# Gates' running sums as rows of the logits' second product; the gated products dealt over six heads

## The chip, the cores and the metric

The kernel runs on one core of a Trainium2 chip. The time is device time in microseconds (us) for one execution; the number compared is the median of several runs. The core has a matrix engine (TensorE, PE in the profile, with PEld for its weight loads), VectorE (DVE), ScalarE (ACT), GpSimd (POOL), and queues that issue DMA transfers (SP's is the one used most). Each engine takes its instructions in the order in which the built kernel has them.

## The reference

One decoder block over a sequence of 1024 tokens and width 1024: forgetting attention with 8 heads of 64, beside a spatial gating branch in chunks of 128 tokens, then a gated feed-forward with a causal convolution. What the change touches is the attention's logits and the branch's output product:

```python
c = jnp.cumsum(log_f, axis=1)                      # running sums of the forget gates, per head
logits = jnp.einsum('bqhd,bkhd->bhqk', qi, k).astype(jnp.float32) * scale
logits = logits + ci[..., None] - c_k
causal = pi[:, None] >= key_pos[None, :]
logits = jnp.where(causal, logits, -jnp.inf)
p = jax.nn.softmax(logits, axis=-1)
...
mix = jnp.concatenate([att, sg], axis=-1)          # sg: the gated branch
h = h + mix @ w_out[layer]
```

The term of the query's own position falls out of the softmax, so the kernel adds only the key's.

## The kernel before

Matrix products are made in a 32-bit format of reduced precision from operands that are split into a high and a low half (`hi`, `lo`); a product is then the sum of three. ScalarE usually makes the high half (`act.copy`, L154 in `split_w`) and VectorE or GpSimd the low half (L160: source minus high half). A product of 512 columns with four blocks of weights is 12 matmuls.

The program runs in this order:

- Input products for the gated branch and the values.
- Four steps of query and key products (`qk_step`, i = 0 to 3; TensorE's line is L402 in `product`), each with weights (`Weights`) whose sums S1 to S4 GpSimd makes (L424 to L426, L432). Queries and keys are stored to DRAM (`qd`, `kd`, L534). Beside the steps run the norm of the gate (`gate_part`: square on ScalarE, reduce, root, reciprocal, and two products with `gms` on VectorE) and the forget gates: `forget`, `forget_sums` and `turn`. These share two small tiles of the tag `gg` (`c` and `r`; two buffers), a tag from which the weights' sum S2 also takes its buffer. `turn`, called at the end of step 0, transposes the running sums on TensorE (L518), copies them negated into `rows`, a part of `c`, and stores them to `ncd` (L520).
- Values and spatial gating; `turn_sg` (L705 to L708) turns the gated branch with TensorE transposes, copies on ScalarE (L707) and subtractions on VectorE (L708).
- The attention, heads 0 to 7. `head_loads` brings the operands of a head two heads ahead. `logits(h, j)` makes a block of 128 queries: two matmuls for up to 512 keys each (L796, L797), then one VectorE reduction (L798) that adds the row `ck`, limits, and finds the minimum `mn`, and an exponential on ScalarE (L800). `ck` is the running sum of the head, broadcast by DMA to 128 partitions; before each block GpSimd sets the keys after the query to a large number in it (affine select, L790). `turn_p` transposes the weights (L813) and splits them (ScalarE L814, VectorE L815), and `values` multiplies them with V (L832, L840, L841). `row_tail` inverts the row sums (L738, L739, L741), and `pair_half` normalizes a pair of heads on GpSimd (L752 to L754; on VectorE for the last pair).
- The gated branch's output product, `sg_out`, is a generator of 16 products (two halves of the weights `wos` by 8 token tiles; TensorE L874 to L876, VectorE L877). The table `FILLS` says after which step (head, step) one product is taken; key (-1, j) is after the logits' block j of head 0, which is made before any step. They lie between the attention's matmuls as filling. The second half's weights are split when the eighth product is done.
- Output product of the attention, for which GpSimd splits weights during the last heads (`wo_load`), and the feed-forward, which is most of the time and not touched.

The scheduler that orders each engine's instructions works from its own estimates; an `after` call fixes one instruction behind another. Before, GpSimd's normalizations and weight splits are fixed behind chosen selects (`sels`).

## Time and profile before

| | |
|---|---|
| median of 3 runs | 1076.82 us (1076.59 to 1077.02) |
| profiled execution | 1076.44 us |
| its span in the trace | 1074.7 us |
| mean granted TensorE clock | 0.998 of full |
| TensorE busy | 1054.8 us, 5013 instructions |
| VectorE busy | 892.9 us, 1303 instructions |
| ScalarE busy | 571.0 us, 985 instructions |
| GpSimd busy | 237.2 us, 219 instructions |

The profile lists the busy time of each engine, the busy shares in slices, the chain of work that ended last, and the costliest groups of instructions with the idle time before them and who ended it. In a timeline row stand the start in us from the span's start, the length (of the whole run of x instructions), engine, line, operation, output tile and input tile with shapes, how many, and in brackets the engine's idle time just before and what ended it. A wait row has engine and line, what was waited for, the total in us, how often, and the longest. PE's matmuls are pipelined: one of 512 columns takes 0.39 us from end to end, but the next starts after 0.23 us.

### The profile page before, as it was taken

The page shows a single profiled execution, that of the slowest core. Times are in us where ns is not written, and L with a number is a line of the kernel's source. Part 1 is how long each engine was busy: PE and PEld are TensorE (multiplying, and loading weights), DVE is VectorE, ACT ScalarE, POOL GpSimd, SP SyncE. Part 2 cuts the span into 40 slices and gives each one's busy share as a digit, 9 for nine tenths or more (in the row PEclk, how much of TensorE's full clock was granted, in tenths as well). Part 3 has the DMA queues.
Part 4 walks back from the last instruction along what each step waited for, and adds up shares of the span by engine and source line. Part 5 has one row for each costly group of instructions (what it writes and reads, how often), then busy time and mean ns, then how long its engine had stood idle before and what let it go on. Part 6 is the DMA issues. An engine that isn't in the chain of part 4 may idle for free.

```text
span 1074.7 us, 14461 instructions
## 1 busy us (share of the span) xinstructions
PE 1054.8 (98%) x5013; PEld 875.8 (81%) x5013; DVE 892.9 (83%) x1303; ACT 571.0 (53%) x985; POOL 237.2 (22%) x219
## 2 busy tenths in 40 slices
PE   9999999989999899999999999999999999999997
PEld 6888788778888788878888888888888888888886
DVE  5985798777777869999899999989988776898774
ACT  6666644456666845764444444444444444454653
POOL 0002134020223651054333333333322000000000
PEclk9999999999999999999999999999999999999999
DMA  9242257957556335132244523223331899433442
GB/s 338 97 140 97 68 159 213 265 165 215 162 177 225 120 128 185 72 118 97 98 137 161 172 69 127 99 98 99 107 118 46 289 327 319 123 95 97 140 125 96
DMA packets 66297, 160.80 MB, mean 150 GB/s; under 512 B 7976, under 2 KB 8240, under 8 KB 66224
## 3 DMA queue, kind: packets, MB, share of 16 engines
q1 hardware_dynamic: 65792, 159.32, 45.5%
q8 instruction: 39, 0.64, 0.2%
q10 hardware_dynamic: 432, 0.57, 0.1%
q14 instruction: 34, 0.28, 0.1%
HBM read 117.06 MB, written 42.80 MB: 149 GB/s over the span
## 4 chain that ended last, share of the span: by engine, by line
PE 74%; DVE 2%; issue 2%; DMA 2%; ACT 2%; POOL 0%; DVEq 0%; ACTq 0%; POOLq 0%; SPq 0%
PE k L1369 19%; PE qa L1117 11%; PE qc L1117 11%; PE qd L1117 11%; PE qb L1117 5%; PE pb L832 2%; PE pb L813 2%; PE pf L874 1%; PE pf L876 1%; PE pf L875 1%; PE pl L796 1%; PE pl L797 1%; DMA raw<-wos 1%; PE pb L1026 1%; PE pb L1028 1%
## 5 line engine op out<-in xcount | busy, mean ns | idle before, releaser
L1369 PE MATMUL k<-whb,wha 128*128 128x512 f32 x924 | 209.7, 389 | 0.0
L1369 PEld LDWEIGHTS k<-whb,wha 128*128 128x128 f32 x924 | 173.3, 188 | 36.2 <-DVE wha L160 0.2
L1117 PE MATMUL qc<-xT,whb 128*128 128x512 f32 x540 | 129.8, 389 | 0.0
L1117 PE MATMUL qa<-xB,wha 128*128 128x512 f32 x528 | 127.2, 390 | 0.0
L1117 PEld LDWEIGHTS qc<-xT,whb 128*128 128x128 f32 x540 | 101.3, 188 | 21.2 <-ACT whb L154 0.2
L1117 PEld LDWEIGHTS qa<-xB,wha 128*128 128x128 f32 x528 | 98.8, 188 | 20.8 <-DVE wha L160 0.4
L154 ACT CAST wha<-sg 128x512 fp32r<-128x512 f32 x77 | 47.7, 622 | 96.9 <-PE k L1369 86.6
L154 ACT CAST whb<-sg 128x512 fp32r<-128x512 f32 x82 | 50.6, 618 | 85.8 <-PE qc L1117 68.5
L160 DVE TENSOR_TENSOR wha<-sg,wha 128x512 fp32r<-128x512 f32 x77 | 52.8, 688 | 41.0 <-ACT wha L154 40.9
L1117 PE MATMUL qd<-xB,whb 128*128 128x512 f32 x264 | 63.8, 389 | 0.5 <-DVE h L1236 0.5
L1117 PE MATMUL qd<-xT,whb 128*128 128x512 f32 x264 | 63.6, 389 | 0.0
L815 DVE TENSOR_TENSOR pt<-pb,pt 128x512 fp32r<-128x512 f32 (+1 forms) x80 | 50.0, 635 | 14.5 <-ACT pt L814 13.4
L160 DVE TENSOR_TENSOR whb<-sg,whb 128x512 fp32r<-128x512 f32 x82 | 58.3, 711 | 4.4 <-ACT whb L154 4.3
L1117 PE MATMUL qb<-xT,whb 128*128 128x512 f32 x252 | 60.8, 389 | 0.0
L1004 POOL TENSOR_TENSOR sg<-raw 128x512 f32<-128x512 f32 x20 | 30.9, 1546 | 134.2 <-DVE whb L160 76.0
L1117 PEld LDWEIGHTS qd<-xB,whb 128*128 128x128 f32 x264 | 49.5, 188 | 11.2 <-issue 0.9
L1117 PEld LDWEIGHTS qd<-xT,whb 128*128 128x128 f32 x264 | 49.5, 188 | 10.3
L1117 PEld LDWEIGHTS qb<-xT,whb 128*128 128x128 f32 x252 | 47.3, 188 | 9.8
L814 ACT CAST pt<-pb 128x512 fp32r<-128x512 f32 (+1 forms) x80 | 42.5, 539 | 20.6 <-PE pb L813 14.7
L832 PE MATMUL pb<-pt,V 128*128 128x256 f32 x320 | 51.4, 285 | 1.3 <-DVE pt L815 1.2
L790 POOL TENSOR_SCALAR_AFFINE_SELECT x<-x 128x128 f32<-128x128 f32 x64 | 19.9, 312 | 129.7 <-DVE mn L798 77.4
L1007 POOL TENSOR_TENSOR sg<-sg,raw 128x512 f32<-128x512 f32 x20 | 33.3, 1664 | 64.1 <-DVE whb L160 64.1
(396 smaller groups left out, 2305.7 us busy)
## 6 DMA issues: line engine op xcount, KB each, us to landing
raw<-wup SPq DMA_DIRECT2D x44, 512.0 KB, 3.7
sg<-hx SPq DMA_DIRECT2D x77, 256.0 KB, 2.6
hx<-hs SPq DMA_DIRECT2D x44, 256.0 KB, 3.8
hx<-ca SPq DMA_DIRECT2D x35, 256.0 KB, 2.0
xT<-wdn SPq DMA_DIRECT2D x28, 256.0 KB, 4.3
raw<-wqk SPq DMA_DIRECT2D x8, 512.0 KB, 3.6
qd<-G SPq DMA_DIRECT2D x16, 256.0 KB, 3.5
kd<-G SPq DMA_DIRECT2D x16, 256.0 KB, 3.3
```

What stands on the lines that cost most here:

```text
L154: act.copy(h, src)
L160: return eng.tensor_tensor(out=l, in0=src, in1=f32(h), op=ALU.subtract)
L790: sels[h].append(pool.affine_select(out=ck[:, qs], in_=ck[:, qs], pattern=[[-1, P]], compare_op=ALU.is_ge, fill=BIG, base=0, channel_multi ...
L796: seq(pe.matmul(ps[:, c:e], A[:, qs], B[:, c:e], start=True, stop=False))
L813: seq(pe.transpose(ptr[:, c:c + P], tj[jj][:, k * P:(k + 1) * P], ident))
L814: act.copy(pt[:, 0, 0:w], ptr[:, 0:w])
L815: dve.tensor_tensor(out=pt[:, 1, 0:w], in0=ptr[:, 0:w], in1=f32(pt[:, 0, 0:w]), op=ALU.subtract)
L832: seq(pe.matmul(po[0][:, oo:oo + n], lhs, pt[:, s, o:o + n], start=(k == 0 and s == 0), stop=(s == 1 and half)))
L1004: pool.tensor_tensor(out=s[0], in0=a21, in1=a22, op=ALU.add)
L1007: pool.tensor_tensor(out=s[3], in0=s[1], in1=a12, op=ALU.add)
L1117: pe.matmul(ps, w[:, wi, ks], xb[:, xi, k, :], start=(first and n == 0), stop=(n == 11), skip_group_check=True)
L1369: pe.matmul(banks[bk + m], xh[:, xi, ms], wh[:, wi, :], start=(first and p_ == 0 and n == 0), stop=(p_ == NP - 1 and n == 2), skip_group_c ...
```

## The change

- The mask leaves the logits' running sums: a constant tile `msk` (zeros, and in its last 128 columns the triangle `maskb`), built once, is what the reduction adds, shifted by where its slice begins. The 64 affine selects are gone.
- The running sums become rows of the second product. Before, the two products were [qh; ql] by [kh; kl] and [qh; ql] by [kl; kh]. Now the first is [qh; ql] by [kh; kh], the second [qh; 1; 1] by [kl; c high; c low], with 66 rows. Number and width of the matmuls are the same; the term of both low halves is left out.
- `turn` splits the sums: high half by ScalarE, low half by a new VectorE operation, both in the tile `r` over `tri` and `ones`, two stores to `ncd`. A row of ones is stored to `oned`.
- `head_loads`: the keys' high half twice, the queries' high half, the two rows of sums, the keys' low half, and, for the first two heads, the rows of ones. The broadcast load of 512 KB is gone.
- `FILLS`: after the three in head 0's logits, before 3, 2, 3, 2, 3 products in heads 0 to 4, now 3, 2, 2, 2, 2, 2 in heads 0 to 5.
- The second half's weights of `sg_out` get their low halves on GpSimd, not VectorE.
- The `after` calls behind selects are gone with the selects.

```diff
-FILLS = {(-1, j): 1 for j in (5, 3, 0)} | {(h, s): 1 for h in range(5) for s in ((0, 2, 4), (1, 3))[h % 2]}
+FILLS = {(-1, j): 1 for j in (5, 3, 0)} | {(h, s): 1 for h in range(6) for s in ((0, 2, 4), (1, 3), (0, 3), (0, 2), (0, 3), (0, 2))[h]}
...
-    ncd = drm.tile([8, 1024], F32, name="ncd")
+    ncd = drm.tile([2, 8, 1024], F32, name="ncd")
+    oned = drm.tile([2, 1024], F32, name="oned")
...
         act.copy(ones, one128)
+        sp.dma_start(out=oned.rearrange("s (t p) -> (s t) p", p=P), in_=f32(ones[0:16, :]))
...
         def turn():
             pe.transpose(ps[0:64, 192:320], z, ident)
-            act.activation(rows, ps[0:64, 192:320], AF.Copy, scale=-1.0)
-            sp.dma_start(out=ncd.rearrange("h (t p) -> (h t) p", p=P), in_=rows)
+
+            rh, rl = r[0:64, 0:P], r[0:64, P:2 * P]
+            act.activation(rh, ps[0:64, 192:320], AF.Copy, scale=-1.0)
+            dve.scalar_tensor_tensor(out=rl, in0=ps[0:64, 192:320], scalar=-1.0, in1=f32(rh),
+                                     op0=ALU.mult, op1=ALU.subtract)
+            for s, t in enumerate((rh, rl)):
+                sp.dma_start(out=ncd[s].rearrange("h (t p) -> (h t) p", p=P), in_=f32(t))
...
-    sels = [[] for _ in range(8)]
+
+    idr = sb("t01", [P, 1024])
+    msk = idr[:, 0:512].bitcast(BF16)
+    pool.memset(msk[:, 0:1024 - P], 0.0)
+    pool.tensor_copy(msk[:, 1024 - P:1024], maskb)
...
-        rt = sb("t01", [8, P])
+        rt = idr[0:8, 640 + P * hh:640 + P * (hh + 1)]
...
-            s = sels[2 * p + 3][o.start // 512 * 3:]
-            after(tc, pool.tensor_tensor(out=f[:, 0, o], in0=f[:, 0, o], in1=f[:, 1, o], op=ALU.mult), s[0])
-            after(tc, pool.tensor_copy(t[:, 0, o], f[:, 0, o]), s[1])
-            after(tc, pool.tensor_tensor(out=t[:, 1, o], in0=f[:, 0, o], in1=f32(t[:, 0, o]), op=ALU.subtract), s[2])
+            pool.tensor_tensor(out=f[:, 0, o], in0=f[:, 0, o], in1=f[:, 1, o], op=ALU.mult)
+            pool.tensor_copy(t[:, 0, o], f[:, 0, o])
+            pool.tensor_tensor(out=t[:, 1, o], in0=f[:, 0, o], in1=f32(t[:, 0, o]), op=ALU.subtract)
...
-    cks, b2s = sb("x2", [P, 2, 1024]), sb("x2", [P, 2, 1024], F32R)
+    a2s, b2s = sb("x2", [P, 2, 1024], F32R), sb("x2", [P, 2, 1024], F32R)
...
-        sp.dma_start(out=f32(ab[:, 1, :]), in_=kd[h].rearrange("s d t -> (s d) t"))
-        sp.dma_start(out=cks[:, hh, :], in_=ncd[h:h + 1, :].to_broadcast((P, 1024)))
-        sp.dma_start(out=f32(b2s[0:64, hh, :]), in_=kd[h, 1])
-        loads[h] = sp.dma_start(out=f32(b2s[64:128, hh, :]), in_=kd[h, 0])
+        for s in range(2):
+            sp.dma_start(out=f32(ab[s * 64:s * 64 + 64, 1, :]), in_=kd[h, 0])
+        sp.dma_start(out=f32(a2s[0:64, hh, :]), in_=qd[h, 0])
+        if h < 2:
+            sp.dma_start(out=f32(a2s[64:66, hh, :]), in_=oned)
+        sp.dma_start(out=f32(b2s[64:66, hh, :]), in_=ncd[:, h, :])
+        loads[h] = sp.dma_start(out=f32(b2s[0:64, hh, :]), in_=kd[h, 1])
...
-        sels[h].append(pool.affine_select(out=ck[:, qs], in_=ck[:, qs], pattern=[[-1, P]], compare_op=ALU.is_ge,
-                                          fill=BIG, base=0, channel_multiplier=1))
...
-            seq(pe.matmul(ps[:, c:e], A[:, qs], B2[:, c:e], start=False, stop=True))
-        dve.tensor_tensor_reduce(out=t, in0=ps[:, 0:n], in1=ck[:, 0:n], scale=1.0, scalar=lim[:, 0:1],
+            seq(pe.matmul(ps[:, c:e], A2[:, qs], B2[:, c:e], start=False, stop=True))
+        dve.tensor_tensor_reduce(out=t, in0=ps[:, 0:n], in1=msk[:, 1024 - n:1024], scale=1.0, scalar=lim[:, 0:1],
...
                 if hf == 0 and tt == 7:
-                    whs = split(nxt, "dve")
+                    whs = split(nxt, "pool")
```

More of the change, by code (lines that the diff above doesn't have):

```diff
@@ L460, in forget @@
         wfa, sel = c[:, 0:128].rearrange("p (a b) -> p a b", b=8), c[0:64, 128:136]
-        bfb, z, e, rows = c[:, 136:144], c[:, 144:208], c[:, 208:272], c[0:64, 272:400]
-        tri, ones, lh, ll = r[:, 0:P], r[:, P:2 * P], r[:, 256:320], r[:, 320:384]
+        bfb = c[:, 136:144]
+        tri, ones = r[:, 0:P], r[:, P:2 * P]
         sp.dma_start(out=wfa[:, 0:8, :], in_=wf)
@@ L490, in forget_sums @@
     def forget_sums(c, r, zr):
-        sel, bfb, z, e, rows = c[0:64, 128:136], c[:, 136:144], c[:, 144:208], c[:, 208:272], c[0:64, 272:400]
+        sel, bfb, z, e = c[0:64, 128:136], c[:, 136:144], c[:, 144:208], c[:, 208:272]
         tri, ones, lh, ll = r[:, 0:P], r[:, P:2 * P], r[:, 256:320], r[:, 320:384]
@@ L781, in logits @@
         i, jj, hh = j // 2, j % 2, h % 2
-        A, B, ck, B2 = abs_[h][:, 0, :], abs_[h][:, 1, :], cks[:, hh, :], b2s[:, hh, :]
+        A, B, A2, B2 = abs_[h][:, 0, :], abs_[h][:, 1, :], a2s[0:66, hh, :], b2s[0:66, hh, :]
         w1, w2 = (2 * i + 1) * P, (2 * i + 2) * P
@@ L897, in wo_load @@
                 src = wr[:, hf * 512:hf * 512 + 512]
-                s = sels[6][4 * k + 2 * hf:] if k < 2 else sels[7][7:] * 2
-                after(tc, pool.tensor_copy(w[hf][:, 0], src), s[0])
-                after(tc, pool.tensor_tensor(out=w[hf][:, 1], in0=src, in1=f32(w[hf][:, 0]), op=ALU.subtract), s[1])
+                pool.tensor_copy(w[hf][:, 0], src)
+                pool.tensor_tensor(out=w[hf][:, 1], in0=src, in1=f32(w[hf][:, 0]), op=ALU.subtract)
             wo.append(w)
```

## The prediction

> **What bounds the kernel now.** I read the page's head first, then the busy time by stage (windows), then TensorE's waits in the attention, and last the timeline at the four places that the change touches.

> ```profile
> span 1074.7 us, 14461 instructions
> PE 1054.8 (98%) x5013; PEld 875.8 (81%) x5013; DVE 892.9 (83%) x1303; ACT 571.0 (53%) x985; POOL 237.2 (22%) x219
> ```

> TensorE is busy 98% of the span, and the change leaves its 5013 instructions as they are in number and width. So only 20 us of TensorE's idle time can be won in the whole program, and whatever makes TensorE wait is paid in full. The stages (columns: length, PE, PEld, DVE, ACT, POOL busy, granted clock, DMA share, GB/s):

> ```profile
> 128.00:138.00 10.00, 10.00 (x46) 8.17 (x45) 10.00 (x22) 6.42 (x12) 5.62 (x4) 1.00 0.56 144
> 138.00:148.00 10.00, 10.00 (x46) 8.28 (x45) 10.00 (x12) 3.36 (x6) 5.71 (x4) 1.00 0.73 184
> 222.00:240.00 18.00, 16.68 (x93) 14.15 (x94) 12.96 (x29) 13.22 (x28) 6.71 (x11) 1.00 0.33 111
> 300.00:355.00 55.00, 54.22 (x356) 48.14 (x355) 41.68 (x86) 36.22 (x80) 16.23 (x32) 1.00 0.62 197
> 355.00:387.00 32.00, 26.96 (x208) 24.68 (x208) 26.31 (x58) 26.35 (x59) 21.68 (x31) 1.00 0.28 93
> ```

> Three things to see. While the query and key products of the second step run (128 to 148), VectorE is full as well: an instruction more there, or one in another place, reaches TensorE at once. At the attention's start TensorE is idle for 1.3 us. And from 300 to 355, where most heads have gated products as filling, 0.8 us in 55 are idle, but from 355 on, where none is left (the end of head 5, heads 6 and 7), 5 us in 32. That last stretch is what the new dealing aims at.

> ```profile
> DVE t L798 <- POOL x L790: 0.3, 1, 0.3
> L790 POOL TENSOR_SCALAR_AFFINE_SELECT x<-x 128x128 f32<-128x128 f32 x64 | 19.9, 312 | 129.7 <-DVE mn L798 77.4
> ```

> In these last heads (the waits of 350 to 390) VectorE waits once, 0.3 us, for GpSimd's selects; what TensorE waits for there is VectorE, by the three rows under (d). All 64 selects are 19.9 us on an engine that is 22% busy.

> **The change part by part.** The order of the instructions on each engine is that of the built kernel, set against the one before; the times below are on the clock of the trace of before.

> *(a) Running sums as rows, step 1 of the query/key products.* The low half of the sums now lies where `tri` and `ones` lay, so that `gg` tile lives until the stores. The sum S2 of the next weights (L425) must take the other `gg` tile and wait for TensorE's transpose in `turn` (L518).

> ```profile
> 130.24 1.62 POOL L425 TENSOR_TENSOR gg<-raw,raw 128x512 f32<-128x512 f32 x1
> 135.68 1.06 ACT L44 ACTIVATE pt<-G 128x1024 f32<-128x1024 f32 x1
> 136.42 0.27 PE L518 MATMUL ps<-ident,gg 128*64 128x128 f32 x1
> 136.45 3.00 PE L402 MATMUL qb<-H,whl 128*128 128x512 f32 x12
> 139.56 0.68 DVE L44 SCALAR_TENSOR_TENSOR G<-G,t 128x512 f32<-128x512 f32 x1
> 140.16 1.21 DVE L44 TENSOR_REDUCE gms<-pt 128x16 f32<-128x1024 f32 x1
> 141.43 1.28 ACT L44 ACT_TABLE_LOAD   x1
> 144.49 3.95 DVE L44 TENSOR_TENSOR G<-G,gms 128x1024 f32<-128x1024 f32 x2
> 145.20 2.15 POOL L425 TENSOR_TENSOR gg<-raw,raw 128x512 f32<-128x512 f32 x1
> 147.45 2.88 PE L402 MATMUL qc<-V,whl 128*128 128x512 f32 x12
> ...
> 220.94 2.40 ACT L154 CAST whl<-raw 128x512 fp32r<-128x512 f32 x4 [5.88 <-DMA raw<-wos]
> 226.26 1.27 DVE L798 CUSTOM_DVE_ANT_0 t<-pl,x,lim 128x1024 f32<-128x1024 f32 x1
> ```

> Before, S2 was ready at 131.9 and TensorE took its product at 136.45. After, S2 runs on GpSimd from 136.7 to 138.3. ScalarE has in its order: the square (one cast earlier than before, to 136.35), the rows' copy (to 137.1), the table load (to 138.4), the root (to 138.7; copy and root are small, and I give each the 0.3 of the transpose), and only then S2's high half (0.6, as each of the four of 220.94; to 139.35). TensorE meanwhile does the 12 products of `qa` (2.73, to 139.4), then two, two and four matmuls that need high halves alone (to 141.3), then it needs S2's low half. VectorE reaches that at 142.0 to 142.7: two low halves (to 136.9), the reduce (138.1), a difference, the new low half of the sums and a scaling (139.7), the reciprocal (140.05; this and the low half at 0.3), the first product with `gms` (1.3 to 2.0), the low half (0.68). TensorE waits 0.7 to 1.4. From there to the difference that frees `qc` VectorE has eight operations of 0.68 and the second product with `gms`, so `qc<-V` starts at 148.7 to 150.1 in place of 147.45. The spread is the price of the `gms` products: 1.98 each in the pair's row, with a GpSimd sum beside them (145.20), or 1.27, as the 1024-wide reduction of 226.26 has it, with no sum on GpSimd beside it. In the new order GpSimd's next sum waits until VectorE's low half of `whl` for `qa`, behind both, so GpSimd is idle then. I take +1.4, near the lower end, and keep 1.2 to 2.6. [...] The second store of the sums, that of `ones`, and each head's small load of sums on SP's queue lie ahead of stores and weights that are due over 5 us later, and a head's loads fall from about 2 MB to 1.5: nothing, at worst 0.3.

> *(b) The attention's start.* Here ScalarE's order decides. Before, the four high halves of the first gated weights (L154, the row of 220.94) stand ahead of the copies of the turned gate (L707). After, the first four copies come first, then three of the weights' casts; the fourth stands behind a copy, the table load, two exponentials, three copies and a third exponential.

> ```profile
> 221.64 5.01 POOL L160 TENSOR_TENSOR whl<-raw,whl 128x512 fp32r<-128x512 f32 x4 [3.80 <-ACT whl L154]
> 222.15 1.53 PE L705 MATMUL pb<-ident,A 128*128 128x128 f32 x12 [1.93 <-DVE V L44]
> 223.25 2.04 ACT L707 CAST G<-pb 128x512 fp32r<-128x512 f32 x4
> 226.98 1.28 ACT L800 ACT_TABLE_LOAD   x1
> 227.60 0.50 PE L796 MATMUL pl<-x 128*128 128x512 f32 x1 [0.44 <-DVE mn L798]
> 228.28 1.15 ACT L800 ACTIVATE t<-t,mn 128x1024 f32<-128x1024 f32 x1
> 228.40 0.40 PE L874 MATMUL pf<-whl,G 128*128 128x512 f32 x1
> 229.43 1.03 ACT L800 ACTIVATE t<-t,mn 128x896 f32<-128x896 f32 x1
> 231.13 0.39 PE L796 MATMUL pl<-x 128*128 128x512 f32 x1
> 231.40 0.94 ACT L800 ACTIVATE t<-t,mn 128x768 f32<-128x768 f32 x1
> 236.47 0.33 PE L796 MATMUL pl<-x 128*128 128x128 f32 x1 [0.73 <-DVE mn L798]
> 239.55 1.80 PE L813 MATMUL pb<-ident,t 128*128 128x128 f32 x15
> ```

> The second copy can't start before the transposes of 222.15, so the four end at 224.3 (0.51 each). Three casts (0.60) end at 226.1, a copy at 226.6, the table load at 227.9, the exponentials of 1024 and 896 at 229.05 and 230.1, three copies at 231.65, the exponential of 768 at 232.6; the fourth cast ends at 233.2, and its low half on GpSimd (1.25) at 234.45. TensorE starts its first gated product at 228.3, as before, has nine of twelve matmuls done at 230.35, and stands: 2.85 us for the high half, one matmul, 1.0 us for the low half. The product ends at 234.9, not 231.13: 3.8 us late. What is late next: the wait of 0.73 before the last logits stays, since VectorE's addition for the second product stands ahead of the reduction it waits for, and the turning of head 0 begins at about 243.4 in place of 239.55. The 0.44 at 227.60 goes, as the reduction now stands ahead of a subtraction; it is in this sum already. (b) is +3.8. Lower end 2.6: the cast 0.5 earlier, the 0.73 gone; upper end 4.6, with another copy's time or two.

> *(c) The low halves of the second half's weights go from VectorE to GpSimd.*

> ```profile
> 278.00 0.68 DVE L841 TENSOR_TENSOR H<-pb,H 64x512 f32<-64x512 f32 x1
> 279.36 1.39 DVE L160 TENSOR_TENSOR whl<-raw,whl 128x512 fp32r<-128x512 f32 x2
> 283.20 0.55 PE L813 MATMUL pb<-ident,t 128*128 128x128 f32 x3 [0.68 <-DVE pt L815]
> 284.94 1.30 POOL L752 TENSOR_TENSOR H<-H 128x512 f32<-128x512 f32 x1 [0.44 <-DVE H L841]
> 285.78 0.40 PE L874 MATMUL pf<-whl,G 128*128 128x512 f32 x1
> ```

> VectorE loses four such operations (2.7 us), so the wait of 0.68 at 283.20 goes: I take −0.55. GpSimd's order is a normalization of head 1 (1.30, waits for L841, 278.7), a low half, a copy, a low half, a subtraction, two low halves: by 1.25 to 1.30 each and 0.6 for the copy, as ScalarE's they end at 281.3, 283.1, 285.7 and 286.9. The product that needs them starts at about 285.1 and uses the third at 286.5 and the fourth at 287.2. It fits, by 0.3 us; the margin is thin, and gives a rival.

> *(d) Six heads, and no selects.* Heads 2 and 4 have two products in place of three, head 5 has two in place of none.

> ```profile
> 358.80 0.63 PE L813 MATMUL pb<-ident,t 128*128 128x128 f32 x4 [0.73 <-DVE pt L815]
> 362.13 0.71 PE L832 MATMUL pb<-pt,V 128*128 128x256 f32 x4 [0.58 <-DVE pt L815]
> 365.75 0.27 PE L739 MATMUL pb<-ident,rs 128*8 128x128 f32 x1 [1.51 <-DVE rs L738]
> ```

> These three waits are VectorE's lag behind TensorE in head 5 and at its end. A product there is 2.73 us of TensorE (228.40 to 231.13) and one addition of VectorE (0.68), so two give VectorE 4 us to catch up: the first two waits and half of the third go, −2.0. Heads 2 and 4 pay 0.4, since in them too a product fewer lets VectorE fall behind. Net −1.6; ends −2.4 and −0.6. Heads 6 and 7 have no filling either way. The selects gone: −0.3, the one wait of VectorE in a stretch where TensorE in turn waits for it; ends −1.0 and 0.

> Sum: +1.4 +3.8 −0.55 −1.6 −0.3 = +2.75. The profiled execution took 1076.44 (span and 1.74 around it), 0.4 below the median of 1076.82; on the median the forecast is 1079.6. Its own range, from the ends of the terms where most is likely to fall together, is 1077.6 to 1081.6.

> **The rivals.**
> - *Faster: the waits at the start don't form.* If ScalarE's fourth cast is over by 230.35 and S2 is not late, what remains is −0.44 at the start, −0.55, −1.6 and −0.3, with +0.3 for the sums: −2.6, 1074.2. For it speaks that 5 us are idle in the last heads; against it that ScalarE takes its instructions in their order, and the row of 231.40 stands ahead of the cast.
> - *No change to be seen: the new waits and the filling cancel.* (a) and (b) at their lower ends (+3.8), the rest at −3.2 (the filling at −2.4): 1077.4. For it: the waits at the heads' ends are long enough (5.0 us idle). A change here of under 0.2%, 2.15 us, I call none.
> - *Slower still: GpSimd becomes what is late at (c).* If the normalization, first in its queue, starts after 281 and not at 278.7, since head 1's row sums or L841 come later, all four low halves shift by as much as 4 us. It decides from 0.3 us of lateness on; at 3.5 us of delay TensorE waits 3.2, and the gain of 0.55 goes: 1083.3. For it: before, GpSimd did that normalization at 284.94 only; against it: L841's row shows its input ready.
> - *Slower: the clock drops after the wait at (b).* TensorE stands for 3.85 us with one matmul in it; if the next product of 2.73 us then ran at half the clock, it would cost 2.7 more, 1082.3. Before, a wait of 1.93 left the clock at 1.00 in its window (222 to 240). [...]

> **How the numbers follow.** Forecast 0.52, faster rival 0.15, none 0.18, GpSimd late 0.10, clock 0.05. The range 1074.0 to 1083.3 reaches to the middles of the two outer rivals and leaves out half of each, a little over a tenth. Faster by over 0.2% (below 1074.7) is most of the first rival, 0.13; same takes the third case, a share of the forecast's lower end (up to 1079.0) and the rest of the first rival, 0.28; slower is 0.59.

> **What would show it.** In the changed kernel's timeline: TensorE waiting for ScalarE's and then GpSimd's `whl` inside the first gated product, together near 3.8 us; a wait in the second query/key step for VectorE's `whl`, and a later start of its `qc<-V`; no wait at the first pass of a second-half product; and the stretch of the last heads with 3 us idle, not 5. I am wrong if the first gated product runs through without a wait, or if the last heads keep their 5 us.

## The result and the profile after

The changed kernel takes 1083.4 us (median of 6 runs, 1082.14 to 1085.49), the kernel before 1076.88 (6 runs, 1075.86 to 1077.91): ratio 1.0061, 95% interval 1.0048 to 1.0074. It is 6.5 us slower. The profiled execution took 1082.14 with a span of 1080.4; by the traces the loss is 5.7 us. The head of the page, and then busy time by stage with the stretches of before, where all columns are as before:

```profile
span 1080.4 us, 14293 instructions
PE 1057.1 (98%) x5013; PEld 877.6 (81%) x5013; DVE 889.6 (82%) x1300; ACT 571.1 (53%) x985; POOL 221.6 (21%) x161
```

```profile
138.00:148.00 10.00, 9.55 (x42) 7.32 (x41) 9.96 (x16) 4.87 (x10) 2.76 (x3) 1.00 0.63 166
222.00:240.00 18.00, 13.85 (x67) 11.24 (x68) 11.02 (x20) 11.78 (x22) 5.03 (x4) 0.91 0.15 50
300.00:355.00 55.00, 54.30 (x355) 48.06 (x354) 42.24 (x90) 37.77 (x84) 6.37 (x6) 1.00 0.63 172
355.00:387.00 32.00, 27.71 (x203) 25.11 (x202) 25.72 (x56) 24.92 (x56) 20.81 (x22) 1.00 0.44 141
```

GpSimd is freed as meant (58 instructions fewer). No gain from that shows by itself: in the last heads of the kernel before, VectorE waited only 0.3 us for GpSimd's selects. TensorE has its 5013 instructions, but is busy 2.3 us longer: some of them ran at a lower clock. Where, the row of 222 to 240 tells: 4.15 us idle where there were 1.32, and a granted clock of 0.91 in place of 1.00. The other three rows move by less: 0.45 us idle in the query/key step where there was none, 0.7 in the heads with filling (0.8 before), 4.3 in the last heads (5.0 before). (The program is 5.8 us late by then; stretches moved by as much give the same 0.7 and 4.3.) The timeline of the changed kernel at the attention's start, 222 to 246:

```profile
223.25 1.57 ACT L714 CAST G<-pb 128x512 fp32r<-128x512 f32 x3 [2.01 <-PE pb L712]
224.70 1.67 ACT L155 CAST whl<-raw 128x512 fp32r<-128x512 f32 x3
226.93 1.28 ACT L812 ACT_TABLE_LOAD   x1
228.68 0.50 PE L886 MATMUL pf<-whl,G 128*128 128x512 f32 x1 [0.37 <-DVE G L715]
230.40 1.53 ACT L714 CAST G<-pb 128x512 fp32r<-128x512 f32 x3
231.82 0.95 ACT L812 ACTIVATE t<-t,mn 128x768 f32<-128x768 f32 x1
232.75 0.61 ACT L155 CAST whl<-raw 128x512 fp32r<-128x512 f32 x1
233.41 0.50 PE L886 MATMUL pf<-whl,G 128*128 128x512 f32 x1 [2.38 <-ACT whl L155]
233.44 1.27 POOL L161 TENSOR_TENSOR whl<-raw,whl 128x512 fp32r<-128x512 f32 x1 [4.27 <-ACT whl L155]
234.76 0.51 PE L887 MATMUL pf<-whl,G 128*128 128x512 f32 x1 [0.84 <-POOL whl L161]
235.92 0.63 PE L809 MATMUL pl<-x,x 66*128 66x512 f32 x1
242.26 0.33 PE L808 MATMUL pl<-x 128*128 128x128 f32 x1 [0.74 <-DVE mn L810]
245.36 1.80 PE L825 MATMUL pb<-ident,t 128*128 128x128 f32 x15
```

Between the third and the fourth cast stand, on ScalarE, the table load, copies and three exponentials, and TensorE waits 2.38 for it and 0.84 for its low half: 3.22 us. The matmul of 235.92 then takes 0.63 from end to end, where one of 512 columns took 0.39. The windows show why (the last three columns are the granted clock, the DMA share and GB/s):

```profile
234.00:236.00 2.00, 1.24 (x4) 1.01 (x5) 0.27 (x1) 0.00 (x0) 0.70 (x1) 0.78 0.08 18
236.00:238.00 2.00, 2.00 (x7) 1.67 (x6) 1.45 (x4) 0.17 (x1) 0.00 (x0) 0.50 0.65 243
238.00:240.00 2.00, 2.00 (x9) 1.62 (x8) 0.62 (x2) 1.53 (x4) 0.00 (x0) 0.87 0.20 39
```

At half clock for 0.88 us of the first window, all of the second and 0.52 of the third: 3.4 us, in which 1.7 us of work are lost. Head 0 is turned at 245.36, not 239.55: 5.8 us are lost by here, which is all of the loss that the traces show at the end (5.7). The remaining 835 us of the program add nothing on balance.

Two more places, the second query/key step and the last heads:

```profile
136.38 3.00 PE L403 MATMUL qa<-x,wy 128*128 128x512 f32 x12
136.76 1.29 POOL L426 TENSOR_TENSOR gg<-raw,raw 128x512 f32<-128x512 f32 x1 [4.96 <-PE ps L520]
138.13 1.90 POOL L433 TENSOR_TENSOR raw<-gg,raw 128x512 f32<-128x512 f32 x1
139.17 1.94 DVE L44 TENSOR_TENSOR G<-G,gms 128x1024 f32<-128x1024 f32 x1
141.77 2.57 PE L403 MATMUL qb<-H,whl 128*128 128x512 f32 x10 [0.45 <-DVE whl L44]
144.05 1.21 DVE L44 TENSOR_TENSOR G<-G,gms 128x1024 f32<-128x1024 f32 x1
148.26 2.88 PE L403 MATMUL qc<-V,whl 128*128 128x512 f32 x12
...
364.28 0.63 PE L825 MATMUL pb<-ident,t 128*128 128x128 f32 x4 [0.15 <-DVE pt L827]
367.59 0.71 PE L844 MATMUL pb<-pt,V 128*128 128x256 f32 x4 [0.55 <-DVE pt L827]
371.22 0.27 PE L750 MATMUL pb<-ident,rs 128*8 128x128 f32 x1 [1.50 <-DVE rs L749]
```

The step waits 0.45 for the late sum and its `qc<-V` begins 0.8 us later than before; at the attention's first transposes behind the 1.93 us wait 0.4 of it is left (222.55 against 222.15). Of head 5's three waits (0.73, 0.58, 1.51 before) only the first shrank.

### The profile page after: what moved, and what is told of

It is laid out like the page before. It is cut to its first block, busy times and chain, and to the rows that moved or that the text cites. A ratio compares the mean times of both kernels' runs of the same rounds, so it can differ in the third digit from the quotient of the medians.

```text
span 1080.4 us, 14293 instructions
## 1 busy us (share of the span) xinstructions
PE 1057.1 (98%) x5013; PEld 877.6 (81%) x5013; DVE 889.6 (82%) x1300; ACT 571.1 (53%) x985; POOL 221.6 (21%) x161
## 4 chain that ended last, share of the span: by engine, by line
PE 76%; DVE 3%; ACT 2%; issue 1%; POOL 0%; DVEq 0%; ACTq 0%
PE k L1380 19%; PE qa L1128 11%; PE qc L1128 11%; PE qd L1128 11%; PE qb L1128 5%; PE pb L844 3%; PE pb L825 2%; PE ps L259 2%; PE pl L808 1%; PE pl L809 1%; PE pf L886 1%; PE pf L887 1%; PE pf L888 1%; PE pb L1037 1%; PE pb L1039 1%
## 5 line engine op out<-in xcount | busy, mean ns | idle before, releaser
L1015 POOL TENSOR_TENSOR sg<-raw 128x512 f32<-128x512 f32 x20 | 30.9, 1547 | 138.7 <-DVE whb L161 80.6
L844 PEld LDWEIGHTS pb<-pt,V 128*128 128x128 f32 x320 | 44.2, 190 | 5.1 <-PE pb L825 2.2
```

Source lines behind the costliest of these rows:

```text
L844: seq(pe.matmul(po[0][:, oo:oo + n], lhs, pt[:, s, o:o + n], start=(k == 0 and s == 0), stop=(s == 1 and half)))
L1015: pool.tensor_tensor(out=s[0], in0=a21, in1=a22, op=ALU.add)
```

## The experiments

Two theories stood at first: the order of the casts on ScalarE is the whole loss, once as waits and once as clock; or the loss is spread over the change's parts. The kernel before, run beside each group of them, had medians of 1077.0 to 1077.2 (9 to 21 runs). The ratios, with their 95% intervals, are against it; they are not quotients of the two medians and differ from those by up to 0.0007.

### The casts' place, and the clock

**The weights' split earlier in the program.** The split (ScalarE's four casts and their low halves) is called ahead of `turn_sg`, not after the first three blocks of logits.

```diff
         whs = split(load(0), "pool")
+        yield
...
     head_loads(1)
+    next(filler)
     turn_sg(0)
```

> The changed kernel with the first half's weights taken up ahead of the turning of the gate, so that the fourth high half stands with the other three and ahead of the table load and the exponentials on ScalarE. Theory (the place of this one cast makes TensorE stand 3.2 us, and the clock falls after it): no wait in the first gated product, granted clock 1.00 throughout, about 5.3 us less than the changed kernel, near 1078. Rival (the loss lies in the new logits and heads, and the wait only shows it earlier): the wait goes, but the time stays above 1082.

Measured: 1082.59 us (1081.9 to 1083.59), ratio 1.0057 (1.0044 to 1.0069). The stall only moved. Timeline:

```profile
224.41 0.59 ACT L714 CAST G<-pb 128x512 fp32r<-128x512 f32 x1 [2.16 <-PE pb L712]
226.60 2.18 ACT L155 CAST whl<-raw 128x512 fp32r<-128x512 f32 x4
232.27 2.02 ACT L714 CAST G<-pb 128x512 fp32r<-128x512 f32 x4
233.70 0.47 PE L887 MATMUL pf<-whl,G 128*128 128x512 f32 x1 [2.78 <-DVE G L715]
```

The four casts run together, but behind the gate's first copies, in ScalarE's busy time; before, they ran from 220.94, while it waited for the transposes anyway. Now the second four copies come behind two exponentials, and TensorE waits 2.78 us for them. In this execution the clock is at 0.50 twice, behind the 1.93 us wait (223.9 to 227.3) and behind this one (234.2 to 237.6). So it seems not to be the one cast as such, but some 2 us of ScalarE's work that have left a free place; the run with before's order, below, puts them back there.

**The first matmuls twice.** The changed kernel makes the nine matmuls of the first gated product that need only the three early casts a second time.

```diff
-                for k in range(4):
+                first = [0, 1, 2] * 1 if hf == 0 and tt == 0 else []
+                for n, k in enumerate(first + [0, 1, 2, 3]):
...
```

> The changed kernel with the first nine matmuls of the first gated product made twice, so that TensorE works 2.05 us longer in the place where it would stand; the fourth cast stays late. Theory (a long idle stretch lowers the granted clock): the product ends no later than before, idle is 1.2 us and not 3.2, the clock stays at 1.00, and 1.7 to 2 us are saved, near 1081.5. Rival (the lower clock has another cause, or costs nothing): no saving, 1083.4, or more by the added 2.05 us.

Measured: 1081.79 us (1081.4 to 1082.14), ratio 1.0048 (1.0035 to 1.006): 1.6 less than the changed kernel, with nine matmuls more. Its timeline, and one of its windows:

```profile
233.21 0.49 PE L888 MATMUL pf<-whl,G 128*128 128x512 f32 x1 [0.36 <-ACT whl L155]
234.56 0.50 PE L889 MATMUL pf<-whl,G 128*128 128x512 f32 x1 [0.85 <-POOL whl L161]
```

```profile
236.00:238.00 2.00, 2.00 (x10) 1.62 (x10) 1.53 (x5) 1.11 (x3) 0.00 (x0) 1.00 0.55 202
```

The cast comes as late as ever (TensorE goes on at 233.21, not 233.41), but TensorE has work meanwhile, and the clock stays at 1.00. Work without a use bought 1.6 us: that is the clock's part of the loss. It agrees with the 1.7 us of work that the windows above give.

**Before, with the fourth cast late.**

```diff
+                if lo_eng == "pool" and len(whs) == 3:
+                    c4 = act.copy(w[:, 0], wr)
+                    after(tc, c4, exs[2])
...
```

> The kernel before with its fourth high half fixed behind the third exponential, as the changed kernel has it; nothing else is changed. Theory: TensorE stands over 3 us in the first gated product, the clock falls to about half for some 3.4 us, and the time is 4.5 to 5.5 us above the kernel before, near 1082. Rival (the wait costs only together with the other parts of the change): under 2 us above it.

Measured: 1083.7 us (1082.77 to 1085.08), ratio 1.0069 (1.0055 to 1.0083). Timeline and window:

```profile
232.13 0.49 PE L879 MATMUL pf<-whl,G 128*128 128x512 f32 x1 [2.65 <-ACT whl L859]
233.48 0.79 PE L880 MATMUL pf<-whl,G 128*128 128x512 f32 x1 [0.85 <-POOL whl L861]
```

```profile
234.00:236.00 2.00, 2.00 (x7) 1.63 (x6) 0.69 (x1) 0.00 (x0) 0.00 (x0) 0.50 0.37 131
```

One cast in another place costs the kernel before the whole 6.7 us, with the same two waits and the same half clock. Nothing else of the change is in this kernel.

**The change with before's order at this place.** The split is called ahead of `turn_sg` here too. The four casts are fixed ahead of the first copy of the gate, the sixth copy ahead of the first exponential (in this run's trace all eight stand there, before it was six), and the reduction of the first logits, block 7, behind the first four subtractions.

```diff
+            if hf == 0 and c == 0:
+                after(tc, x, casts[-1])
...
+            if hf == 1 and c == 1:
+                after(tc, exs[0], x)
...
+        if (h, j) == (0, 7):
+            after(tc, d, subs[3])
```

> The changed kernel with the first half's weights taken up ahead of the turning, and the order at the attention's start fixed: ScalarE's four casts ahead of the copies of the turned gate, all copies ahead of the table load, VectorE's first reduction behind the first four subtractions. The run with the casts merely called earlier did not have this: there they ran after the first copies, and ScalarE was late with the second four copies. Theory (ScalarE must use its free 2 us before the transposes for the casts; else TensorE stands and the clock falls): no wait over 1 us in the first gated product, head 0's turning begins near 240 and not at 245.4, clock 1.00 behind it, 5.4 us less than the changed kernel, near 1078. Rival (some 5 us are lost by the new logits anyway and would show elsewhere): above 1081.

Measured: 1077.36 us (1076.84 to 1079.62, 11 runs), ratio 1.0007 (0.9998 to 1.0016). 6.0 us of the loss are gone.

**What set the order.** Between the loads of head 0 and head 1, sync's queue takes the first weights of `wos`; nothing is fixed by hand.

```diff
-        whs = split(load(0), "pool")
+        raw0 = load(0)
+        yield
+        whs = split(raw0, "pool")
...
     head_loads(0)
+    next(filler)
     head_loads(1)
```

> After, with the load of the output weights' first rows issued between the loads of head 0 and those of head 1, not behind both; nothing is pinned. Theory (in the kernel after each head has 6 or 7 loads in the sync queue instead of 5, so the weights land some 3 us later, and ScalarE's order follows from that: the casts fall behind the gate's copies and the fourth behind the exponentials): all four casts stand ahead of the first copy of the gate as in the kernel before, the 2.4 and 0.8 us waits of the first product go, head 0's row tail is turned at about 246 instead of 252.1, and the time is 1076.5 to 1078 us. Rival (the order comes from the shorter reductions' and copies' place in the program, not from the loads): the casts stay behind, time 1082 to 1084.

Measured: 1077.24 us (1076.53 to 1079.1, 11 runs), ratio 1.0007 (0.9998 to 1.0016). One row of sync's queue in the kernel before, then in the changed one; then three of this run:

```profile
209.30 1.53 SPq L850 DMA_DIRECT2D raw<-wos  x2
```

```profile
212.35 2.96 SPq L862 DMA_DIRECT2D raw<-wos  x2
```

```profile
205.15 2.21 SPq L862 DMA_DIRECT2D raw<-wos  x2
215.79 2.17 ACT L155 CAST whl<-raw 128x512 fp32r<-128x512 f32 x4
240.46 1.80 PE L825 MATMUL pb<-ident,t 128*128 128x128 f32 x15
```

In the changed kernel a head brings six loads, with the ones seven, where it brought five, and the weights behind them go out 3 us later; the built order then has the casts behind the gate's copies. Issued 7 us earlier, the same casts stand ahead of all copies, in ScalarE's free time, and there is no wait inside the first product. So the time of this load sets the casts' order. That it was late because of the added small loads is read from the queue: head 1's loads begin at 204.64 in both kernels, and the weights follow 4.7 us later before and 7.7 after. No run changes the number of loads alone.

### The other parts

**The sums' rows elsewhere**, in free columns of the tile `c`, so that the `gg` tile is free as early as before: once in the changed kernel, once with the loads moved.

```diff
-            rh, rl = r[0:64, 0:P], r[0:64, P:2 * P]
+            rh, rl = c[0:64, 0:P].bitcast(F32R), c[0:64, 272:400].bitcast(F32R)
```

> The changed kernel with the two halves of the running sums in free columns of the other small tile, so that the weights' sum S2 needs no wait for the transpose, and the order of the products in the second query/key step is as before. Theory from the traces (the detour costs 0.4 us by the start of the attention): 0.4 us less, not to be told from none. By the prediction's term: 1.4 us less, near 1082.

> The kernel of the run ahead of it with the rows of the gates' sums written to free columns of another constant tile, so that they wait for no reader of the triangle and the ones. If the first term of the prediction's sum is worth what the traces showed (0.2 to 0.4 us), the time is 0.2 to 0.4 us under the run ahead, about 1076.8; if it is worth the 1.4 us that the prediction gave it, about 1075.8.

Measured: 1081.76 us (1081.01 to 1084.09, 5 runs), ratio 1.0051 (1.0039 to 1.0064); and 1076.19 us (1075.42 to 1077.54, 11 runs), ratio 0.9997 (0.9988 to 1.0006). The second pair, 11 runs against 11 on one chip, gives 1.05 us; the first, with few and scattered runs, 1.6. Both are nearer to the prediction's term of 1.4 than to the 0.2 to 0.4 that the traces let expect. In the trace of the second the step is as before:

```profile
136.05 3.00 PE L403 MATMUL qb<-H,whl 128*128 128x512 f32 x12
147.05 2.88 PE L403 MATMUL qc<-V,whl 128*128 128x512 f32 x12
```

From the one row to the other are 11.0 us, as before (136.45 to 147.45), against 11.88 in the changed kernel: 0.9. This last kernel has the lowest median of all, 0.8 under before, and its interval holds 1: a better version, if it is one, by less than can be told.

**The dealing and the low halves**, each by itself: the old `FILLS` in the changed kernel, the new `FILLS` in the one before, and the second half's low halves back on VectorE.

```diff
-                    whs = split(nxt, "pool")
+                    whs = split(nxt, "dve")
```

> The changed kernel with the products dealt over five heads as before. By the traces, which leave 4.99 us idle from the third head on in place of 5.82, 0.8 us more, near 1084.2. By the prediction's term 1.6 us more, 1085. Rival (the dealing does nothing here): no change.

> The kernel before with the new dealing over six heads alone. By the traces 0.8 us less, near 1076.1; by the prediction's term 1.6 us less, 1075.3; rival: no change or slower, since heads 2 and 4 lose a product that hid VectorE's lag.

> The changed kernel with the second half's low halves on VectorE as before. By the prediction's term (VectorE is relieved) 0.55 us more. By the trace (the waits of 1.05 and 0.47 in head 1 come from ScalarE's lateness, with VectorE itself idle before them): no change, or up to 0.7 less.

Measured: old dealing 1085.2 us (1084.37 to 1085.92), ratio 1.0077 (1.0064 to 1.0089), 1.8 over the changed kernel; new dealing in before 1076.61 (1075.07 to 1078.12, 11 runs), ratio 0.9997 (0.9988 to 1.0006), 0.5 under before; low halves on VectorE 1085.59 (1084.12 to 1086.21), ratio 1.008 (1.0066 to 1.0094), 2.2 over the changed kernel. The second can't be told from none. The runs of the first and third scatter by 1.5 to 2 us, and not all of their loss comes from the edit: in their traces the transposes of head 0's row sums come at 253.19 and 253.18, against 252.09 in the changed kernel, 1.1 us late ahead of what these edits touch; up to there the clock was at half for 6.8 us in all and not for 3.4. Behind it the old dealing loses 1.0 us by head 5's end, and the low halves on VectorE 1.2 in head 1. With the old dealing the changed kernel has, in head 5:

```profile
369.71 0.71 PE L844 MATMUL pb<-pt,V 128*128 128x256 f32 x4 [0.58 <-DVE pt L827]
373.33 0.27 PE L750 MATMUL pb<-ident,rs 128*8 128x128 f32 x1 [1.51 <-DVE rs L749]
```

The wait for the row sums is 1.51 with the old dealing and 1.50 with the new: two products in head 5 do not touch it. With the low halves on VectorE a wait grows in head 1, from 0.47 to this:

```profile
291.54 0.55 PE L825 MATMUL pb<-ident,t 128*128 128x128 f32 x3 [1.32 <-DVE pt L827]
```

### Does before lose clock too?

The profile of the run with before's order shows a half clock (0.50 from 224.5 to 227.9) although its longest wait there is 1.93 us, the one ahead of the attention that before also has:

```profile
222.00:224.00 2.00, 0.13 (x1) 0.13 (x2) 1.82 (x4) 1.81 (x4) 1.24 (x2) 1.00 0.33 126
224.00:226.00 2.00, 2.00 (x13) 2.00 (x14) 1.02 (x2) 1.92 (x4) 2.00 (x3) 0.63 0.03 9
```

Twelve kernels' profiles have this wait at 1.93 or 1.94 us. In four the clock fell behind it (early split, before's order, and both changed dealings), in eight it stayed at 1.00. To see whether that costs time on average, useless transposes were put into the wait, 12 and then 8.

```diff
-            for t in range(4):
+            again = [0, 1, 2, 3] * (12 // 4 if (hf, c) == (0, 0) else 0)
+            for t in again + [0, 1, 2, 3]:
```

> The kernel of the run ahead with the first four turnings of the gate issued four times, the first three without a use (12 more transposes of 128x128), in the 1.9 us in which TensorE waits ahead of the attention. [...] Rival (the wait of 1.9 us costs no clock): the same time, or up to 0.5 us longer by what the extra transposes put off.

> Before, with the same 12 transposes more in the same wait of 1.93 us, and nothing else. If in part of its runs the kernel before loses clock behind this wait, 0.3 to 1.5 us less on average and runs that lie closer together (before: 1075.2 to 1078.7); if the wait never costs it clock, the same time or up to 0.5 us more.

> Before, with the first four turnings of the gate issued three times (8 more transposes of 128x128) in the 1.93 us wait. Unlike the 12, these 8 leave the first output product in the bank that it has in the kernel before, so the wait at the end of the attention should not come. Theory (in part of its runs the kernel before loses clock behind the 1.93 us wait): 0.3 to 1.0 us less on average, about 1076.4, and runs closer together than before's 1075.1 to 1079.3. Rival (the wait never costs clock): the same time, or up to 0.4 us more.

> The kernel with the load between the two heads' loads and the sums' rows elsewhere (1076.2), with the same 8 transposes more in its 1.94 us wait. Theory: 0.3 to 1.0 us less, about 1075.6, and runs closer together than 1075.4 to 1077.5. Rival: 1076.0 to 1076.6.

Measured: with 12, in the kernel with loads and sums moved (1076.19 without them), 1080.33 us (1079.31 to 1082.58), ratio 1.0035 (1.0022 to 1.0047), and in before 1086.39 (1084.38 to 1088.0), ratio 1.0091 (1.0077 to 1.0105); with 8, in before 1077.85 (1076.15 to 1079.77, 11 runs), ratio 1.0005 (0.9996 to 1.0015), and with loads and sums moved 1076.9 (1076.15 to 1077.75, 11 runs), ratio 0.9998 (0.999 to 1.0007). All four miss the theory that the clock behind this wait costs time on average. The 12 shortened the wait to 0.62, and then other places changed: in before this wait behind the attention, with the clock at 0.50 from 390.7 to 397.5,

```profile
391.40 0.77 PE L1027 MATMUL pb<-whl,A 128*128 128x512 f32 x1 [4.92 <-DVE H L842]
```

as the first output product got a buffer whose reader, VectorE's last addition, stood behind a transfer (VectorE waited 3.13 us for it, to 389.85). The 8 kept that buffer, and in before a wait of 1.07 us for VectorE came at 419 (0.88 at 416 with loads and sums moved). What a drop behind the 1.93 us wait costs on average stays open: no run shows that closing it gains.

## Why the prediction was wrong

The direction was right; the size was not, 2.75 us forecast and 6.5 measured, just beyond the top of the range. By its steps:

```profile
282.24 0.83 ACT L826 CAST pt<-pb 128x384 fp32r<-128x384 f32 x2
282.72 1.02 DVE L827 TENSOR_TENSOR pt<-pb,pt 128x384 fp32r<-128x384 f32 x2 [0.37 <-ACT pt L826]
283.43 0.47 PE L886 MATMUL pf<-whl,G 128*128 128x512 f32 x1 [1.05 <-DVE pt L827]
```

  VectorE itself waits 0.37 us for the first of two casts of ScalarE, which stand behind two exponentials (280.49 to 282.23). This reading wasn't tested. TensorE never waited for GpSimd there, so that rival fell; that its 1083.3 is near the measured time is chance.
- **(d): mis-sized.** Forecast −1.6 and −0.3 for the selects. With the loads and the sums mended, what remains of (c), (d) and the selects together is −0.8 us against before (1076.19 to 1077.03), which can't be told from none, where the three terms made −2.45. The error is in head 5's waits: the second and half of the third, for the row sums, were to go, and they stayed at 0.55 and 1.50; the last heads have 4.3 us idle, where 3 were forecast. The products lie at the head's first steps, and VectorE's work at the head's end comes after both.

In time: +1.05 for (a), +6.16 for the order at the attention's start, −0.84 for the rest make +6.4 of the 6.5 measured. The three are steps from one kernel to the next, so they had to add up; the sizes are what they tell.

## What to carry to other kernels

When an engine has little to do for a moment, ask what lies in that moment: a few casts there cost nothing, and the same casts after it stood in the way of 6 us. Look at what is issued behind more, smaller loads: with six and seven for a head in place of five it began 7.7 us after head 1's loads, not 4.7, and these 3 us went with another order of ScalarE's instructions. A wait of a busy TensorE cost its length here and, where the clock fell behind it (0.50 for 3.4 us, after 2.55 us of idle time in the 3.4 us before), about 1.6 us more; price both, and add up waits that lie close together.

## What was not expected of the hardware

The granted clock fell to 0.50 for 3.4 us after 3.2 us of waits that a matmul had split in two, and behind one and the same wait of 1.93 us it fell in 4 profiles of 12; in those the wait lay whole inside the 3.413 us ahead of the drop. Twelve transposes in an idle moment of TensorE cost before 9 us through places 170 us further on: in a kernel this full, the buffers' order is part of what is timed.
